# Layer 0 attention: key rank parts in a pool of their own that later holds head 1's operands, head 1 split ahead of the attention loop, rope weights behind each evacuation

## The chip, the cores and the metric

The kernel runs on one core of one Trainium2 chip. The metric is device time in microseconds (us) of one execution. A core has five engines that work side by side and each take their instructions strictly in order: TensorE (PE; its weight loads are listed apart as PEld), VectorE (DVE), ScalarE (ACT), GpSimd (POOL) and SyncE (SP, which here only issues DMA transfers). Matrix products land in PSUM, everything else lives in SBUF, and large arrays stay in HBM.

## The reference

Two decoder layers over 1024 positions of width 1024, each with a token mixer, four memory cross-attention heads beside it, an output projection and a squared-ReLU MLP. The change touches the mixer of layer 0, multi-head latent attention with 12 heads:

```python
proj = hn @ w_in
c_q, c_kv, k_r, q_cross = ...            # ranks 384 and 256, rope key 32, cross queries 256
q = (rmsnorm(c_q, q_norm_g) @ w_uq).reshape(b, s, 12, 96)
q = concatenate([q[..., :64], rope(q[..., 64:], positions)])
kv = (rmsnorm(c_kv, kv_norm_g) @ w_ukv).reshape(b, s, 12, 128)
k_nope, v = kv[..., :64], kv[..., 64:]
k = concatenate([k_nope, broadcast(rope(k_r))])
o = causal_dense_attention(q, k, v)      # softmax(q k / sqrt(96), masked) v
x = x + concatenate([o, cross]) @ w_o
```

## The kernel before

All products are computed at float32 accuracy by splitting each operand into a rounded high part and a residue (`split`: ACT writes the high part, DVE the residue, names ending in h and l) and adding three matmuls: high by high, high by low, low by high. An operand that is "split" therefore costs one ACT and one DVE instruction before PE can use it.

The part around the change, in the order of the program:

- **Input projection and transposes** (`a_in`, `a_cT`). For each of eight token blocks the normalised ranks are transposed by PE, seven blocks of 128 columns and the 32 rope-key columns, into two PSUM tiles `psct`, and split into `cTh`, `cTl`: slices 0 to 2 are the query rank, slices 3 and 4 the rank of keys and values.
- **Values** (`values_of`, PSUM `psv`) and the cross-attention heads.
- **Keys' nope parts** (PSUM `pskn`, six tiles `j` of two heads each, PE lines 118 to 121). A tile is evacuated half by DVE (line 924) and half by ACT (line 925) into `kq`. Two PSUM tiles alternate, so tile `j+2` needs the evacuation of tile `j`. At `j == 1` all nine pieces of the rope weights `wqr` are requested in one go (`load_cols`): SP loads a raw piece `wr` (line 700, two staging buffers), ACT scales it to `wqrh` (line 102), DVE writes the residue `wqrl` (line 103).
- **Rope queries** (`q_rope`, PSUM `psqr`), which need a whole third of `wqr` for each step `kt`, then rotation, transposes `psqt`, and meanwhile the nope weights `wqn`.
- **Query loop** (`q_nope`, PSUM `psqn`, lines 109 to 111), with the row maxima of head 0 in it (`row_max`, PSUM `psx`: PE line 897, DVE lines 901 and 904) and at the end the transpose of the maxima (`max_row`, PSUM `psxt`, PE line 877), whose result becomes row 96 of head 0's query operand.
- **Attention loop**, 12 heads of 12 blocks. A step issues the score matmuls (`pss`, line 1027), the mask on diagonal blocks (DVE line 1035), the exponential `p` (ACT line 1037), for some blocks a split `ph`, `pl`, then the value matmuls `pso` (line 1057) of a block three steps back, with row maxima of the next heads in between. The tables `WHEN` and `ahead` set the order by hand. `masked` holds the last mask and exponential; `tc.issue_after` places what follows behind a given instruction on its engine.
- **Head operands** (`head_tiles(h)`): four loads on SP gather a head's query `q32` and key `k32` (96 rows), which are split into `qh, ql, kh, kl` (lines 99 and 100 as `split` prints them). Three sets `bufs_` rotate over the heads. Set 0 lies in pool `hb`; sets 1 and 2 lie in `hb1`, opened only after the query loop, when `cp` (with `cTh`, `cTl`) and `xq` have been released. So head 1 is split just ahead of the attention loop and head 2 at its seventh step.
- **Denominators**. The last row of `pso` is the sum of a row's probabilities. For groups of 6, 4 and 1 heads (`GRP`), DVE takes the reciprocal (`rc_split`), a DMA writes it out, and `rc_pair` broadcasts it back to 64 partitions a head into `rb`, `[128, 512]` with two buffers: POOL issues these for groups 0 and 1 (line 1109), SP for the last. `rc_mul` multiplies the outputs by it (DVE line 1126). Head 11 is normalised directly from PSUM (`last_o`, reciprocal line 1096 and product line 1097, four pieces).
- **Output projection** (PSUM `pswo`, lines 109 to 111): its stationary operand `x_...` is split per token block, and the first pass needs the high part (L109, L110) before the residue (L111).

The order within an engine comes from a scheduler that places instructions by its own estimate of when they are ready; the order on the chip is then fixed.

Of the kernel before, what the change touches and what calls it, by code (L numbers as in the profile page):

```python
# [19 lines left out]
P = 128  # L20
# [35 lines left out]
def trunk(  # L56
# [670 lines left out]
    def a_cT(t):  # L727
        sl = slice(t * P, (t + 1) * P)
        c = cs_.pop(t)
        pt = [ps1(f"psct{t}_{i}") for i in range(2)]  # L730
        for i in range(7):
            nc.tensor.transpose(pt[i // 4][:, (i % 4) * P : (i % 4 + 1) * P], c[:, i * P : (i + 1) * P], ident)
        nc.tensor.transpose(pt[1][0:32, 3 * P : 4 * P], c[:, CKR : CKR + 32], ident)
        pv = [q.rearrange("p (k c) -> p k c", k=4) for q in pt]
        split(pv[0], cTh[:, 0:4, sl], cTl[:, 0:4, sl])
        split(pv[1][:, 0:1, :], cTh[:, 4:5, sl], cTl[:, 4:5, sl])
        for h in range(4):
            stack_split(pt[1][(h % 2) * 64 : (h % 2) * 64 + 64, (1 + h // 2) * P : (2 + h // 2) * P], qc[:, h, sl], 1.0)
        nc.scalar.activation(krT[:, sl], pt[1][0:32, 3 * P : 4 * P], AF.Copy)

    for k in range(NT + 2):
        if 1 < k < NT:
# [16 lines left out]
    def values_of(t):  # L759
        sl = slice(t * P, (t + 1) * P)  # L760
        ps = [ps1(f"psv{t}_{g}")[:, 0:384] for g in range(2)]
        gs = [slice(g * 384, (g + 1) * 384) for g in range(2)]
        mm3w(ps, [(cTh[:, 3 + kt, sl], cTl[:, 3 + kt, sl], [(wkv[kt][0][:, s], wkv[kt][1][:, s]) for s in gs]) for kt in range(2)])
        nc.scalar.activation(v[:, t, gs[0]], ps[0], AF.Copy)
        nc.vector.tensor_copy(v[:, t, gs[1]], ps[1])

# [144 lines left out]
    krs = raw_tile([32, S], "krs")  # L911
    hb = pool("hb")
    head_bufs(hb, 0)
    head_ones(0)
    nc.vector.tensor_copy(krs, krT)
    for j in range(6):
        if j == 1:
            wqr = rows(wpair(wu, 3, 384, "wqr", "b"), 3)
            for _ in load_cols(mla_w_uq[0], 3, 96, [(wqr, 64, 32)], g_q):
                pass  # L920
        ps = ps2(f"pskn{j}")
        mm3w([ps[:, s] for s in halves],
             [(wkn[kt][0][:, j * P : (j + 1) * P], wkn[kt][1][:, j * P : (j + 1) * P], [(cTh[:, 3 + kt, s], cTl[:, 3 + kt, s]) for s in halves]) for kt in range(2)])
        nc.vector.tensor_copy(kn[j][:, 0:512], ps[:, 0:512])
        nc.scalar.activation(kn[j][:, 512:1024], ps[:, 512:1024], AF.Copy)
# [178 lines left out]

    def rc_pair(c, j, i):

        rb = at.tile([P, 512], F32, tag="rb", bufs=2, name=f"rb{c}_{j}_{i}")
        for e in range(min(2, GRP[c + 1] - GRP[c] - 2 * j)):
            (nc.sync if c == 2 else nc.gpsimd).dma_start(out=rb[e * 64 : e * 64 + 64, :], in_=rc_d[c][2 * j + e, halves[i]].partition_broadcast(64))
        return rb  # L1110

    def rc_split(c):

        n = (GRP[c + 1] - GRP[c]) * NT
        rc = at.tile([48, P], F32, tag="rc", bufs=1, name=f"rc{c}")[:n]
        nc.vector.reciprocal(rc, den[c])
        (nc.sync if c == 2 else nc.gpsimd).dma_start(out=rc_d[c].rearrange("h (t p) -> (h t) p", p=P), in_=rc)
        r_tiles[c] = [(j, i) for j in range((GRP[c + 1] - GRP[c] + 1) // 2) for i in (1, 0)]
        r_tiles[c] = [(j, i, rc_pair(c, j, i)) for j, i in r_tiles[c]]

    def rc_mul(c):

        for j, i, rb in r_tiles.pop(c):
            m = 64 * min(2, GRP[c + 1] - GRP[c] - 2 * j)
            o = qn[GRP[c] // 2 + j][0:m, halves[i]]
            nc.vector.tensor_tensor(o, rb[0:m], o, ALU.mult)
            yield

# [4 lines left out]
    v_tiles(0)  # L1133
    v_full(0)
    mask(wide[0], 1)
    head_tiles(1)

    LV, LB = 3, 5
    NB = len(blocks)
# [60 lines left out]
    at.release()  # L1200
    hb1.release()
    hb.release()
    kvp.release()

# [1106 lines left out]
```

## Time and profile before

| | us |
|---|---|
| median of 3 runs | 2097.34 (2095.71 to 2097.36) |
| the profiled execution | 2098.42 |
| its span (first to last instruction) | 2096.7 |
| PE busy in the span | 2073.6 |
| DVE / ACT / POOL busy | 1473.6 / 1109.1 / 148.9 |
| mean granted TensorE clock | 0.999 |

The stages of the change in this trace: keys' nope parts 175 to 192 us, rope queries 192 to 207, query loop 207 to 235, attention 235 to about 436, output projection from there. A row of the timeline reads: start, duration, engine, line of the kernel, operation, output `<-` inputs by the program's names, shape, count, and in brackets how long the engine had been idle before it and who released it. Since the ends of pipelined matmuls are modelled, the distance between two starts says more than the duration. A row of the table of stretches gives the window, its length, then busy us and count of PE, PEld, DVE, ACT and POOL, the granted clock (1.00 is full), the busy share of the DMA engines and GB/s.

### The profile page before, as it was taken

Reading aid. Unit: us, or ns where it says so; the run is one execution under the profiler, and the core shown is the slowest. Engines: PE = TensorE matmul, PEld = TensorE weight load, DVE = VectorE, ACT = ScalarE, POOL = GpSimd, SP = SyncE. Lnnn points to the kernel's source line nnn. Section 1 sums busy time; section 2 is a strip of 40 time slices with the busy share of each in tenths; the row PEclk is TensorE's granted clock in tenths of the full one; section 3 lists DMA queues with packets and bytes.
Section 4 is the critical chain, followed back from the end, with each engine's and each line's share of the span. In section 5 each row is a group of like instructions: output and inputs, shape, how many; then the busy total and the mean of one; then the engine's idle time right before and its main releaser. Section 6 shows DMA issues by size and latency. Waiting matters only on the chain.

```text
span 2096.7 us, 28899 instructions
## 1 busy us (share of the span) xinstructions
PE 2073.6 (99%) x9744; PEld 1691.1 (81%) x9744; DVE 1473.6 (70%) x2978; ACT 1109.1 (53%) x2396; POOL 148.9 (7%) x265
## 2 busy tenths in 40 slices
PE   8999999999999999999999999999999999999998
PEld 6988777778888888888888878778888888888887
DVE  8766777775977777976658534666977776976565
ACT  7554466656755544444446435776755444444453
POOL 1001001000000000000001133421000000000000
PEclk9999999999999999999999999999999999999999
DMA  6302233342344446944433534542345446945342
GB/s 219 99 1 76 59 69 87 101 147 91 125 153 164 161 146 233 326 140 155 141 116 106 151 92 126 138 138 81 119 163 165 155 141 232 328 148 156 117 120 90
DMA packets 181939, 292.33 MB, mean 139 GB/s; under 512 B 17707, under 2 KB 72096, under 8 KB 181792
## 3 DMA queue, kind: packets, MB, share of 16 engines
q1 hardware_dynamic: 175296, 272.07, 41.4%
q0 software_dynamic: 5168, 15.80, 2.1%
q10 hardware_dynamic: 1328, 2.63, 0.4%
q8 instruction: 76, 1.25, 0.3%
q14 instruction: 71, 0.58, 0.1%
HBM read 187.34 MB, written 81.18 MB: 128 GB/s over the span
## 4 chain that ended last, share of the span: by engine, by line
PE 93%; DVE 3%; ACT 2%; DMA 1%; issue 1%; ACTq 0%; POOL 0%; DVEq 0%
PE psu L1545 6%; PE psu L1547 6%; PE psu L1546 6%; PE psy L1885 6%; PE psy L1884 6%; PE psy L1883 5%; PE psz L1885 4%; PE psz L1884 4%; PE psz L1883 4%; PE psv L1545 4%; PE psv L1547 4%; PE psv L1546 4%; PE pso L1057 3%; PE pswo L109 3%; PE pswo L111 3%; PE pswo L110 3%
## 5 line engine op out<-in xcount | busy, mean ns | idle before, releaser
L99 ACT ACTIVATE g<-i 128x512 fp32r<-128x512 f32 x79 | 49.8, 631 | 103.3 <-PE psy L1884 51.8
L1037 ACT ACTIVATE p<-pss 128x512 f32<-128x512 f32 (+2 forms) x144 | 68.5, 486 | 59.6 <-DVE pss L1035 51.5
L1883 PE MATMUL psy<-g 128*128 128x512 f32 x256 | 100.0, 390 | 0.0
L1884 PE MATMUL psy<-g 128*128 128x512 f32 x256 | 99.7, 389 | 0.0
L1885 PE MATMUL psy<-g 128*128 128x512 f32 x256 | 99.6, 389 | 0.0
L100 DVE TENSOR_TENSOR g<-i,g 128x512 fp32r<-128x512 f32 x79 | 55.3, 700 | 50.2 <-ACT g L99 50.0
L1057 PE MATMUL pso<-p,vf 128*128 128x512 f32 (+3 forms) x214 | 87.9, 492 | 0.3 <-ACT p L1037 0.3
L99 ACT ACTIVATE i<-mr 128x512 fp32r<-128x512 f32 x78 | 47.8, 627 | 73.1 <-PE psu L1546 20.9
L99 ACT ACTIVATE uh<-i 128x512 fp32r<-128x512 f32 x66 | 41.6, 631 | 82.5 <-PE psz L1884 38.3
L100 DVE TENSOR_TENSOR uh<-i,uh 128x512 fp32r<-128x512 f32 x66 | 45.6, 691 | 46.7 <-ACT uh L99 46.7
L904 DVE CUSTOM_DVE_ANT_0 psx<-psx,wide 128x1024 f32<-128x1024 f32 (+6 forms) x88 | 66.7, 760 | 14.2 <-PE psx L897 14.0
L1883 PE MATMUL psz<-g 128*128 128x512 f32 x192 | 74.7, 389 | 0.0
L1884 PE MATMUL psz<-g 128*128 128x512 f32 x192 | 74.7, 389 | 0.0
L1885 PE MATMUL psz<-g 128*128 128x512 f32 x192 | 74.7, 389 | 0.0
L100 DVE TENSOR_TENSOR i<-mr,i 128x512 fp32r<-128x512 f32 x78 | 53.7, 689 | 24.7 <-ACT i L99 24.5
L1444 ACT ACTIVATE mr<-mr,gcol 128x256 f32<-128x256 f32 (+1 forms) x160 | 63.9, 475 | 12.9 <-DMA mr<-in_mlp_w_up_dram 12.9
L1027 PE MATMUL pss<-qh,kh 97*128 97x512 f32 (+2 forms) x144 | 64.4, 448 | 0.3 <-ACT p L1037 0.2
L1027 PE MATMUL pss<-ql,kh 97*128 97x512 f32 (+2 forms) x144 | 61.4, 426 | 0.0
L1765 DVE TENSOR_TENSOR mqq<-mqf,mqq 128x512 f32<-128x512 f32 x64 | 43.2, 688 | 19.6 <-DMA mqf<-in_mlp_w_down_dram 19.6
L1885 PEld LDWEIGHTS psy<-g 128*128 128x128 f32 x256 | 48.1, 188 | 9.9
L1884 PEld LDWEIGHTS psy<-g 128*128 128x128 f32 x256 | 48.1, 188 | 9.9
L1883 PEld LDWEIGHTS psy<-g 128*128 128x128 f32 x256 | 48.1, 188 | 9.8
(662 smaller groups left out, 6838.3 us busy)
## 6 DMA issues: line engine op xcount, KB each, us to landing
i<-hd SPq DMA_DIRECT2D x154, 256.0 KB
hd<-uh SPq DMA_DIRECT2D x76, 256.0 KB
hd<-ul SPq DMA_DIRECT2D x76, 256.0 KB
mr<-in_mlp_w_up_dram SPq DMA_DIRECT2D x36, 512.0 KB
hd<-x SPq DMA_DIRECT2D x72, 256.0 KB
mr<-hd SPq DMA_DIRECT2D x70, 256.0 KB
d<-in_mlp_w_up_dram SPq DMA_DIRECT2D x32, 512.0 KB
mqf<-in_mlp_w_down_dram SPq DMA_DIRECT2D x32, 512.0 KB
```

What stands on the lines that cost most here:

```text
L99: a = nc.scalar.activation(hi, src, AF.Copy)
L100: d = nc.vector.tensor_tensor(lo, src, f32(hi), ALU.subtract)
L904: nc.vector.tensor_tensor_reduce(o, o, k, -1.0, least, ALU.add, ALU.min, accum_out=m)
L1027: return lambda: nc.tensor.matmul(o, a, b, skip_group_check=True, **kw)
L1037: masked[1:] = [nc.scalar.activation(p[:, c0:], ps, AF.Exp, scale=SC).ins]
L1057: mms.append(lambda: nc.tensor.matmul(o, a, b, skip_group_check=True, **kw))
L1545: nc.tensor.matmul(ps, wh[:, k, :], xh[:, k, :], start=p in (1, 2, 5) and k == 0, stop=False, skip_group_check=True)
L1546: nc.tensor.matmul(ps, wh[:, k, :], xl[:, k, :], start=False, stop=False, skip_group_check=True)
L1547: nc.tensor.matmul(ps, wl[:, k, :], xh[:, k, :], start=False, stop=k == 3, skip_group_check=True)
L1883: nc.tensor.matmul(ps, ah[:, j, :], bh, start=start, stop=False, skip_group_check=True)
L1884: nc.tensor.matmul(ps, ah[:, j, :], bl, start=False, stop=False, skip_group_check=True)
L1885: nc.tensor.matmul(ps, al[:, j, :], bh, start=False, stop=k == NP - 1, skip_group_check=True)
```

## The change

- The rank parts of keys and values get a pool `ckv` with `ckh`, `ckl` (two slices each), and `cTh`, `cTl` keep three. `a_cT` groups the transposes as three plus rope key, and four. `values_of` and the key tiles read `ckh`, `ckl`.
- Once the key tiles are done, the four slices of `ckh`, `ckl` serve as head 1's `qh, ql, kh, kl`. Hence `head_tiles(1)` moves into the query loop at `n == 7`. `hb1` holds head 2's set alone; `ckv` and `xq` are released after the attention.
- `head_tiles(2)` moves from step 6 to step 5 of the attention loop, placed behind the mask and exponential of that step.
- The rope weights are no longer requested in one go at `j == 1`, but two pieces behind each ACT evacuation of a key tile.
- `rb` shrinks to 256 columns, still with two buffers, so there are 24 multiplies for 12, and 44 broadcasts for 22.

```diff
+    ckv = pool("ckv", "right")
+    ckh, ckl = [ckv.tile([P, 2, S], F32R, name=f"ck{e}") for e in "hl"]
     cp = pool("cp", "right")
-    cTh = cp.tile([P, 5, S], F32R, name="cTh")
-    cTl = cp.tile([P, 5, S], F32R, name="cTl")
+    cTh = cp.tile([P, 3, S], F32R, name="cTh")
+    cTl = cp.tile([P, 3, S], F32R, name="cTl")
...
-        for i in range(7):
-            nc.tensor.transpose(pt[i // 4][:, (i % 4) * P : (i % 4 + 1) * P], c[:, i * P : (i + 1) * P], ident)
+        at_ = [(0, 0), (0, 1), (0, 2), (1, 0), (1, 1), (1, 2), (1, 3)]
+        for i, (b, o) in enumerate(at_):
+            nc.tensor.transpose(pt[b][:, o * P : (o + 1) * P], c[:, i * P : (i + 1) * P], ident)
...
-        split(pv[0], cTh[:, 0:4, sl], cTl[:, 0:4, sl])
-        split(pv[1][:, 0:1, :], cTh[:, 4:5, sl], cTl[:, 4:5, sl])
+        split(pv[0][:, 0:3, :], cTh[:, :, sl], cTl[:, :, sl])
+        split(pv[1][:, 0:2, :], ckh[:, :, sl], ckl[:, :, sl])
...
     head_bufs(hb, 0)
+    bufs_.append([t[0:97, e, :] for t in (ckh, ckl) for e in range(2)])
     head_ones(0)
...
-        if j == 1:
+        if j == 0:
             wqr = rows(wpair(wu, 3, 384, "wqr", "b"), 3)
-            for _ in load_cols(mla_w_uq[0], 3, 96, [(wqr, 64, 32)], g_q):
-                pass
+            loading = load_cols(mla_w_uq[0], 3, 96, [(wqr, 64, 32)], g_q)
...
         nc.vector.tensor_copy(kn[j][:, 0:512], ps[:, 0:512])
-        nc.scalar.activation(kn[j][:, 512:1024], ps[:, 512:1024], AF.Copy)
+        with tc.issue_after(nc.scalar.activation(kn[j][:, 512:1024], ps[:, 512:1024], AF.Copy).ins):
+            for _ in range(2):
+                next(loading, None)
...
+        if n == 7:
+            head_tiles(1)
         if n == 8:
             max_row(0)
...
-    xq.release()
...
-    for i in (1, 2):
-        head_bufs(hb1, i)
+    head_bufs(hb1, 2)
...
-        rb = at.tile([P, 512], F32, tag="rb", bufs=2, name=f"rb{c}_{j}_{i}")
+        rb = at.tile([P, 256], F32, tag="rb", bufs=2, name=f"rb{c}_{j}_{i}")
...
-        r_tiles[c] = [(j, i) for j in range((GRP[c + 1] - GRP[c] + 1) // 2) for i in (1, 0)]
+        r_tiles[c] = [(j, i) for j in range((GRP[c + 1] - GRP[c] + 1) // 2) for i in (3, 2, 1, 0)]
...
-            o = qn[GRP[c] // 2 + j][0:m, halves[i]]
+            o = qn[GRP[c] // 2 + j][0:m, i * 256 : i * 256 + 256]
...
-    head_tiles(1)
...
-            if j == (0 if h else 6) and h + 2 < H:
+            if h and j == 0 and h + 2 < H:
                 head_tiles(h + 2)
+            if n == 5:
+                with tc.issue_after(masked[0]), tc.issue_after(masked[1]):
+                    head_tiles(2)
...
     hb1.release()
+    ckv.release()
+    xq.release()
```

Three places show how the instructions stand on DVE. The first is the end of head 0's row maxima in the query loop (`psx0_7` is the last block of maxima, `ckh ... <-q32_1` head 1's query residue, `mhl0` the split of the transposed maxima). Before:

```order
433 L934 COPY qn0_1928<-psqn3_1_2429 128x512
434 L901 TENSOR_REDUCE m8_0_2349<-psx0_7_2413 128x1
435 L904 ISA psx0_7_2413,m8_0_2349<-psx0_7_2413,dmask_66,m8_0_2349 128x128
436 L904 ISA m8_0_2349 128x1
437 L100 TENSOR_TENSOR mhl0_2453<-psxt0_2451,mhl0_2453 8x128
```

And in the changed kernel:

```order
431 L939 COPY qn0_1933<-psqn3_1_2434 128x512
432 L904 TENSOR_REDUCE m8_0_2354<-psx0_7_2418 128x1
433 L100 TENSOR_TENSOR ckh_551<-q32_1_2445,ckh_551 96x1024
434 L907 ISA psx0_7_2418,m8_0_2354<-psx0_7_2418,dmask_66,m8_0_2354 128x128
435 L907 ISA m8_0_2354 128x1
436 L100 TENSOR_TENSOR mhl0_2470<-psxt0_2468,mhl0_2470 8x128
```

The residue of head 1's query now stands between the reduction and the masked maximum of the last block. The second place is the first steps of the attention loop. Before:

```order
441 L1130 COPY vf_2518<-v 128x8x64
442 L100 TENSOR_TENSOR ql_2503<-q_1_2536,qh_2502 96x1024
443 L100 TENSOR_TENSOR kl_2505<-k_1_2537,kh_2504 96x1024
444 L1035 TENSOR_TENSOR pss_0_0_2554<-pss_0_0_2554,dmaskT 128x128
...
462 L100 TENSOR_TENSOR pl_0_2_2615<-p_0_2_2612,ph_0_2_2614 128x256
463 L1000 TENSOR_TENSOR vl_2517<-v,vh_2516 128x256
464 L100 TENSOR_TENSOR ql_2507<-q_2_2636,qh_2506 96x1024
465 L100 TENSOR_TENSOR kl_2509<-k_2_2637,kh_2508 96x1024
466 L1035 TENSOR_TENSOR pss_0_3_2651<-pss_0_3_2651,dmaskT 128x128
```

And in the changed kernel:

```order
440 L1135 COPY vf_2530<-v 128x8x64
441 L1040 TENSOR_TENSOR pss_0_0_2554<-pss_0_0_2554,dmaskT 128x128
...
457 L907 ISA psx_5_2641,m_1_2572<-psx_5_2641,wide 128x768
458 L907 ISA m_1_2572 128x1
459 L100 TENSOR_TENSOR ql_2519<-q_2_2621,qh_2518 96x1024
460 L100 TENSOR_TENSOR pl_0_2_2615<-p_0_2_2612,ph_0_2_2614 128x256
461 L100 TENSOR_TENSOR kl_2521<-k_2_2622,kh_2520 96x1024
462 L1005 TENSOR_TENSOR vl_2529<-v,vh_2528 128x256
463 L1040 TENSOR_TENSOR pss_0_3_2651<-pss_0_3_2651,dmaskT 128x128
```

Head 1's two residues are gone from the start; head 2's two stand a little earlier, still ahead of the mask of block `pss_0_3`. The third place is the end of head 11, where its output is normalised (`rq`, `fa`) and the first operand of the output projection (`x_0_3`) is split. Before:

```order
829 L1096 RECIPROCAL rq_4576<-pso_1_4487 64x128
830 L100 TENSOR_TENSOR x_0_3_4637<-qn_1928,x_0_3_4637 128x512
831 L1097 TENSOR_TENSOR fa_101<-pso_1_4487,rq_4576 64x128
832 L1096 RECIPROCAL rq_4576<-pso_1_4487 64x128
833 L100 TENSOR_TENSOR x_0_3_4637<-fa_101,x_0_3_4637 128x256
```

And in the changed kernel:

```order
837 L1102 TENSOR_TENSOR fa_101<-pso_1_4523,rq_4617 64x128
838 L1101 RECIPROCAL rq_4617<-pso_1_4523 64x128
839 L1131 TENSOR_TENSOR fa_101<-rb_0_1_4567,fa_101 64x256
840 L1102 TENSOR_TENSOR fa_101<-pso_1_4523,rq_4617 64x128
841 L1131 TENSOR_TENSOR fa_101<-rb_0_0_4569,fa_101 64x256
842 L100 TENSOR_TENSOR x_0_3_4685<-qn_1933,x_0_3_4685 128x512
843 L100 TENSOR_TENSOR x_0_3_4685<-fa_101,x_0_3_4685 128x256
```

The first residue of `x_0_3` moved behind the last reciprocal, and two of the narrow multiplies stand ahead of it.

More of the change, by code (lines that the diff above doesn't have):

```diff
@@ L730, in a_cT @@
         pt = [ps1(f"psct{t}_{i}") for i in range(2)]
[L731 to L733 removed]
+        at_ = [(0, 0), (0, 1), (0, 2), (1, 0), (1, 1), (1, 2), (1, 3)]
+        for i, (b, o) in enumerate(at_):
+            nc.tensor.transpose(pt[b][:, o * P : (o + 1) * P], c[:, i * P : (i + 1) * P], ident)
+        nc.tensor.transpose(pt[0][0:32, 3 * P : 4 * P], c[:, CKR : CKR + 32], ident)
         pv = [q.rearrange("p (k c) -> p k c", k=4) for q in pt]
[L735 to L736 removed]
+        split(pv[0][:, 0:3, :], cTh[:, :, sl], cTl[:, :, sl])
+        split(pv[1][:, 0:2, :], ckh[:, :, sl], ckl[:, :, sl])
         for h in range(4):
[L738 to L739 removed]
+            stack_split(pt[1][(h % 2) * 64 : (h % 2) * 64 + 64, (2 + h // 2) * P : (3 + h // 2) * P], qc[:, h, sl], 1.0)
+        nc.scalar.activation(krT[:, sl], pt[0][0:32, 3 * P : 4 * P], AF.Copy)
     for k in range(NT + 2):
@@ L762, in values_of @@
         gs = [slice(g * 384, (g + 1) * 384) for g in range(2)]
-        mm3w(ps, [(cTh[:, 3 + kt, sl], cTl[:, 3 + kt, sl], [(wkv[kt][0][:, s], wkv[kt][1][:, s]) for s in gs]) for kt in range(2)])
+        mm3w(ps, [(ckh[:, kt, sl], ckl[:, kt, sl], [(wkv[kt][0][:, s], wkv[kt][1][:, s]) for s in gs]) for kt in range(2)])
         nc.scalar.activation(v[:, t, gs[0]], ps[0], AF.Copy)
@@ L916, in trunk @@
     for j in range(6):
-        if j == 1:
+        if j == 0:
             wqr = rows(wpair(wu, 3, 384, "wqr", "b"), 3)
-            for _ in load_cols(mla_w_uq[0], 3, 96, [(wqr, 64, 32)], g_q):
-                pass
+            loading = load_cols(mla_w_uq[0], 3, 96, [(wqr, 64, 32)], g_q)
         ps = ps2(f"pskn{j}")
         mm3w([ps[:, s] for s in halves],
-             [(wkn[kt][0][:, j * P : (j + 1) * P], wkn[kt][1][:, j * P : (j + 1) * P], [(cTh[:, 3 + kt, s], cTl[:, 3 + kt, s]) for s in halves]) for kt in range(2)])
+             [(wkn[kt][0][:, j * P : (j + 1) * P], wkn[kt][1][:, j * P : (j + 1) * P], [(ckh[:, kt, s], ckl[:, kt, s]) for s in halves]) for kt in range(2)])
         nc.vector.tensor_copy(kn[j][:, 0:512], ps[:, 0:512])
-        nc.scalar.activation(kn[j][:, 512:1024], ps[:, 512:1024], AF.Copy)
+        with tc.issue_after(nc.scalar.activation(kn[j][:, 512:1024], ps[:, 512:1024], AF.Copy).ins):
+            for _ in range(2):
+                next(loading, None)
     wu2 = pool("wu2", "right")
@@ L1105, in rc_pair @@
     def rc_pair(c, j, i):
-        rb = at.tile([P, 512], F32, tag="rb", bufs=2, name=f"rb{c}_{j}_{i}")
+        rb = at.tile([P, 256], F32, tag="rb", bufs=2, name=f"rb{c}_{j}_{i}")
         for e in range(min(2, GRP[c + 1] - GRP[c] - 2 * j)):
-            (nc.sync if c == 2 else nc.gpsimd).dma_start(out=rb[e * 64 : e * 64 + 64, :], in_=rc_d[c][2 * j + e, halves[i]].partition_broadcast(64))
+            (nc.sync if c == 2 else nc.gpsimd).dma_start(out=rb[e * 64 : e * 64 + 64, :], in_=rc_d[c][2 * j + e, i * 256 : i * 256 + 256].partition_broadcast(64))
         return rb
```

## The prediction

> **What bounds the kernel now.** I read the busy table first, then the chain of waits, then the table of stretches, then TensorE's rows wherever its starts stand further apart than its work asks.
>
> ```profile
> PE 2073.6 (99%) x9744; PEld 1691.1 (81%) x9744; DVE 1473.6 (70%) x2978; ACT 1109.1 (53%) x2396; POOL 148.9 (7%) x265
> PE 93%; DVE 3%; ACT 2%; DMA 1%; issue 1%; ACTq 0%; POOL 0%; DVEq 0%
> ...
> 234.70:250.70 16.00, 13.90 (x68) 10.37 (x67) 15.62 (x35) 10.37 (x20) 2.21 (x5) 1.00 0.32 76
> 435.00:445.00 10.00, 9.13 (x35) 6.38 (x34) 9.66 (x21) 7.69 (x18) 0.00 (x0) 0.83 0.62 228
> ```
>
> TensorE (PE) is busy for 99% of a span of 2096.7 us and holds 93% of the chain. The change takes no matmul away, so it can only move PE's holes. The third and fourth rows are the two stretches in which VectorE (DVE, the fifth figure) is nearly full (15.62 of 16.00 us, 9.66 of 10.00) and PE is not: the start of attention and its end. All terms below are hole sizes, and each hole is the distance between two PE starts less the distance that such a matmul normally has. That normal distance is 0.23 us for 512 columns (191.25 to 191.48 in the rows below) and 0.17 for 384.
>
> **Part A: rope weights behind each evacuation.**
>
> ```profile
> 186.58 0.50 PE L118 MATMUL pskn<-cTh,wknh 128*128 128x512 f32 x1 [1.09 <-ACT kq L925]
> 191.25 0.39 PE L118 MATMUL pskn<-cTh,wknh 128*128 128x512 f32 x1
> 191.48 0.39 PE L119 MATMUL pskn<-cTl,wknh 128*128 128x512 f32 x1
> ...
> 192.16 0.33 PE L109 MATMUL psqr<-wqrh,cTh 128*128 128x384 f32 x1
> 192.33 0.34 PE L110 MATMUL psqr<-wqrl,cTh 128*128 128x384 f32 x1
> ```
> ```profile
> 185.65 0.40 ACT L102 ACTIVATE wqrh<-wr,gcol 128x128 fp32r<-128x128 f32 x1 [1.89 <-DMA wr<-in_mla_w_uq_dram]
> 185.95 0.58 ACT L925 ACTIVATE kq<-pskn 128x512 f32<-128x512 f32 x1
> ...
> 191.66 0.33 SPq L700 DMA_DIRECT2D wr<-in_mla_w_uq_dram  x1
> 193.95 0.51 ACT L102 ACTIVATE wqnh<-wr,gcol 128x256 fp32r<-128x256 f32 x1 [0.27 <-DMA wr<-in_mla_w_uq_dram]
> ...
> 182.69 1.06 ACT L99 ACTIVATE kh<-k 96x1024 fp32r<-96x1024 f32 x1 [0.68 <-DMA k<-kq]
> ```
>
> Today ScalarE (ACT) stands 1.89 us in front of a rope-weight piece that has not landed, the evacuation of a key tile queues behind it, and PE loses about 1.1 us at 186.58. In the change the evacuations come first, so this hole should go: −1.1. The price is that the nine pieces start behind the first evacuation of a key tile instead of ahead of all of them, with only two staging buffers. A piece needs its load (issued 191.66, used 193.95: 2.3 us, the shortest I see; pieces that queue take up to about 3), a 0.40 us scaling on ACT, and a 0.35 us residue on DVE before the buffer is free again.
>
> The late one is the last piece. In the change ACT first splits head 1's key into the rank parts' own space, which PE reads until its last pskn matmul, about 190.8 (192.16 less the hole, less one more matmul). That split takes 1.06 us, the seventh and eighth piece stand behind it on ACT, the ninth can be loaded only when the seventh's residue is done: 190.8 + 1.06 + 0.40 + 0.35 = 192.6, load issued, 2.6 us on its way, 0.40 scaling: about 195.6. PE starts the rope queries at about 190.9 and first runs the two finished thirds for three token blocks, 18 matmuls of 0.17 us, until 194.0. So it waits about 1.6 us for the third. **A: −1.1 + 1.6 = +0.5.** Bounds: −1.1 if the load is early enough, +2.0 if the ninth piece takes 3.2 us and its residue is waited for too. What is late next is the nope weights, by the same 2 to 3 us; but the rope queries stand in front of their first use (90 matmuls' work on PE in that stage), so I cost that at nothing; if that cover is gone it is at most the same 2 us again. The regrouped transposes are the same eight and the same 640 columns in two evacuations: nothing.
>
> **Part B: head 1 is split inside the query loop.**
>
> ```profile
> 226.85 1.09 DVE L901 TENSOR_REDUCE m<-psx 128x1 f32<-128x896 f32 x1
> 227.98 0.36 DVE L904 CUSTOM_DVE_ANT_0 psx<-psx,dmask,m 128x128 f32<-128x128 f32 x1
> ...
> 228.03 0.39 PE L111 MATMUL psqn<-cTh,wqn2l 128*128 128x512 f32 x1
> 228.46 0.27 PE L877 MATMUL psxt<-ident,m 128*8 128x128 f32 x1
> ...
> 237.91 1.21 DVE L100 TENSOR_TENSOR kl<-k,kh 96x1024 fp32r<-96x1024 f32 x1
> ```
>
> The transpose of head 0's maxima (228.46) already starts 0.2 us late: it needs the masked maximum that DVE begins at 227.98. The change puts head 1's query residue, the same shape as the 1.21 us row, exactly between the reduction and that mask. PE executes in order, and its order is unchanged here, so the next query matmuls wait behind the transpose: **+1.2**, bounds 0 (the piece slips into idle DVE time before the reduction) and +1.3. Its four loads and two row copies also move forward on SyncE's queue, between loads of rope weights; each load takes that queue 0.33 us (191.66), and I cost the two row copies, which wait for the rank parts to be free, within A's bounds.
>
> **Part C: start of attention.**
>
> ```profile
> 236.56 0.39 PE L1027 MATMUL pss<-qh,kl 97*128 97x512 f32 x1
> 237.29 0.73 PE L897 MATMUL psx<-kh,qh 96*128 96x512 f32 x2 [0.34 <-ACT kh L99]
> ...
> 239.84 0.33 PE L1027 MATMUL pss<-qh,kl 97*128 97x384 f32 x1
> 240.50 0.70 PE L1057 MATMUL pso<-p,vf 128*128 128x512 f32 x1 [0.32 <-ACT p L1037]
> ...
> 247.45 0.47 PE L1057 MATMUL pso<-pl,vh 128*128 128x256 f32 x1
> 249.30 0.33 PE L897 MATMUL psx<-kh,qh 96*128 96x128 f32 x1 [1.38 <-ACT p L1037]
> ```
> ```profile
> 236.69 1.29 DVE L100 TENSOR_TENSOR ql<-q,qh 96x1024 fp32r<-96x1024 f32 x1
> ...
> 246.38 1.21 DVE L100 TENSOR_TENSOR ql<-q,qh 96x1024 fp32r<-96x1024 f32 x1
> 247.51 1.21 DVE L100 TENSOR_TENSOR kl<-k,kh 96x1024 fp32r<-96x1024 f32 x1
> 248.65 0.29 DVE L1035 TENSOR_TENSOR pss<-pss,dmaskT 128x128 f32<-128x128 f32 x1
> ```
>
> The holes are 0.5 us (236.56 to 237.29, less 0.23), 0.5 us (239.84 to 240.50, less 0.17) and about 1.6 us (247.45 to 249.30). The first two are head 1's own splits, the third is the mask at 248.65 standing behind head 2's. The change takes 1.29 + 1.21 = 2.5 us of DVE work (and as much of ACT) out of a stretch in which DVE never rests. Head 2's stay but start earlier, each behind one more short operation, so the backlog at 247 should be 2.5 us smaller and a hole of 1.6 can close. The sum of holes is 2.6; I take **−2.3**, as head 2's splits may still leave a rest of the third. Bounds: −2.6 (all three close) and −1.0 (only the first two, since head 2's splits still stand before that mask).
>
> **Part D: the denominators in pieces of 256 columns.**
>
> ```profile
> L1109 POOL DMA_DIRECT2D rb<-rcd x20: 516/523/732, 349.2 to 423.1; - x20
> ...
> DMA to landing us min/median/max: 2.7/2.9/3.4
> ```
> ```profile
> 353.15 0.69 DVE L1126 TENSOR_TENSOR qn<-rb,qn 128x512 f32<-128x512 f32 x1 [2.27 <-DMA rb<-rcd]
> ...
> 364.94 0.69 DVE L1126 TENSOR_TENSOR qn<-rb,qn 128x512 f32<-128x512 f32 x1 [0.70 <-DMA rb<-rcd]
> ...
> 246.04 0.42 DVE L1000 TENSOR_TENSOR vl<-v,vh 128x256 fp32r<-128x256 f32 x1
> ...
> 367.08 0.68 PE L897 MATMUL psx<-kh,qh 96*128 96x512 f32 x2 [0.93 <-DVE m L904]
> ```
>
> Twelve multiplies of 0.69 us become 24 of about 0.42 (the row at 246.04 has that width): 12 × (0.84 − 0.69) = 1.8 us more DVE work, spread over 74 us of a kernel in which DVE is busy for 70%. POOL issues 40 broadcasts of 0.52 instead of 20, in a stretch where it is nearly empty. The real cost is the round trip: still two buffers, so each piece waits for the multiply two before it, then 2 × 0.52 of issue and 2.9 of flight, 4 us; DVE waits in order, with masks queued behind it. Before, the waits at 353.15 and 364.94 are such ones, and PE's 0.93 at 367.08 follows the second. From the pace of the masks I expect four further DVE waits of 0.3 to 1.2 us in group 0, one directly ahead of a row-maximum that PE waits for. **D: +0.5**, bounds 0 and +1.5.
>
> **Part E: end of the last head.**
>
> ```profile
> 440.43 0.63 PE L110 MATMUL pswo<-woq,x 128*128 128x512 f32 x1
> 440.86 0.63 PE L111 MATMUL pswo<-woq,x 128*128 128x512 f32 x1
> ...
> 439.80 0.62 DVE L100 TENSOR_TENSOR x<-qn,x 128x512 fp32r<-128x512 f32 x1
> 440.45 0.28 DVE L1097 TENSOR_TENSOR fa<-pso,rq 64x128 f32<-64x128 f32 x1
> 440.77 0.96 DVE L1096 RECIPROCAL rq<-pso 64x128 f32<-64x128 f32 x1
> ```
>
> The first L111 matmul (440.86) needs the residue of the first output-projection tile, which DVE finishes at 440.42. In the change it stands behind the fourth reciprocal (0.96), two products (0.28 each) and two of the four narrow multiplies (0.42 each). Added to 439.80, less what overlaps, it ends at about 442.4, so PE waits **+1.6** at that matmul. Bounds: +0.8 (PE runs here at half rate, 0.43 us from start to start, and a hole inside the slow stretch costs half) and +3.3 (a clock of 0.83 over 10 us is 3.4 us at half rate, so 1.7 us lost, and the hole brings that once more).
>
> The row of the ten microseconds from 435 shows a mean granted clock of 0.83, whereas the stretch with the 1.6 us hole at 248 keeps 1.00, so a longer hole alone doesn't lower it. The Trainium skill ("TensorE: Matmul & The Clock Gate", section "Part 1: The HAM clock gate") says that the clock halves after an idle window of about 3.4 us and returns after as long a busy one. By that rule a hole of 1.6 us slows nothing, as at 248, and E is the hole itself; the slow ten microseconds after 435, in which PE was busy for 9.13, don't fit it.
>
> **The sum.** A +0.5, B +1.2, C −2.3, D +0.5, E +1.6: **+1.5 us**. The profiled execution took 2098.42 us, 1.1 above the median of 2097.34 of the runs shown; a hole costs both the same, so I forecast 2097.34 + 1.5 = **2098.8 us**. Lower bounds of all five together give −2.9 (−1.1, 0, −2.6, 0, +0.8), upper ones +7.1 (2.0, 1.3, −1.0, 1.5, 3.3).
>
> **Rivals.**
> 1. *The gain stays.* The start of attention closes wholly and the other places absorb their delays: DVE is idle for 30% of the span. −1.1 in A with no late ninth piece, B and D nothing, C −2.6, E +0.8: −2.9, 2094.4. Against it: B and E sit where PE already waits, so nothing covers them. Chance 0.12.
> 2. *The clock at the end decides (slower).* If the wait at the first L111 falls before the clock has recovered, another stretch at half rate follows, and each costs the 1.7 us worked out above. With two of them, E is 1.6 + 3.4 = 5.0 and the sum 1.5 + 3.4 = +4.9, 2102.2. [...] For it: the clock does fall here today; against: 248 shows such a hole without a fall. Chance 0.14.
> 3. *The broadcasts' round trip.* Twelve more pieces with two buffers: if half of them hold a mask up for 1 us that PE then waits for, D is +6 and the sum +7.0, 2104.3. Against: of the two DVE waits quoted, 2.27 and 0.70 us, only the shorter one has a PE hole behind it. Chance 0.10.
> 4. *It doesn't do what it says.* Head 1's splits only move from one place where PE waits for DVE to another (B eats C), and the rope weights bring their own hole. This is nearly my sum; with C at −1.0 it is +2.8, 2100.1, still inside what counts as no change. I count it with the forecast.
>
> **How the numbers follow.** A difference of 0.2%, 4.2 us, is about what a measurement of this kernel can tell from no change. Forecast with rival 4: 0.64, all within. Rival 1 (0.12) ends 1.3 us inside the lower edge; small holes that I don't list carry it over in half of the cases, and the rest of it is no change: 0.07 faster. Rival 2 (0.14) lies just beyond the upper edge: 0.10 slower, 0.04 no change. Rival 3 is slower with all its 0.10. So faster 0.07, same 0.73, slower 0.20. The range takes in rivals 1 and 2, and not rival 3: 2093.5 to 2103.5.
>
> **What would show it.** In the changed profile: no wait of pskn for the evacuation near 186, but one of psqr for a rope weight near 194; the transpose of the maxima about 1.2 us after the matmul ahead of it; PE starts 0.17 to 0.23 apart between 236 and 250; a multiply waiting for its broadcast ahead of a row maximum between 350 and 375; the first L111 of the output projection 1 to 2 us later relative to the L110 ahead of it. I am wrong if PE's holes between 175 and 250 shrink by over 3 us in all, or if those after 435 grow by over 4.

## The result, and the profile after

The change makes the kernel slower: median 2106.99 us (2103.74 to 2107.54, six runs) against 2096.7 us (2095.66 to 2097.6, six runs) of the kernel before, a ratio of 1.0045 with a 95% interval of 1.0035 to 1.0056. The forecast was 2098.8, the range ended at 2103.5. The profiled execution took 2106.43 us with a span of 2104.6, 7.9 more than the span of 2096.7 before. The medians differ by 10.3: the profiled execution before was itself 1.7 us above the median of that kernel in this comparison, and the profiled one of the change 0.6 below its own.

The page of the changed kernel, its busy table and its chain of waits:

```profile
PE 2075.8 (99%) x9744; PEld 1692.1 (80%) x9744; DVE 1472.8 (70%) x2990; ACT 1108.7 (53%) x2396; POOL 158.6 (8%) x285
...
PE 91%; DVE 3%; DMA 3%; ACT 2%; issue 1%; POOL 0%; ACTq 0%; DVEq 0%; SPq 0%; POOLq 0%
```

PE has the same matmuls, and DVE about the same work. PE's share of the chain fell from 93% to 91% and DMA's rose from 1% to 3%. So the time went into waits that end with a transfer. The table of what PE waited for, in the changed kernel (total us, times, longest):

```profile
PE psx L900 <- DVE m L907: 4.2, 3, 2.9
PE pswo L111 <- DVE x L100: 1.7, 1, 1.7
PE pso L1062 <- ACT ph L99: 1.5, 2, 1.0
PE psqt L957 <- POOL fa L332: 1.3, 1, 1.3
...
PE psxt L880 <- DVE m L907: 1.0, 1, 1.0
```

The longest wait of the kernel, 2.9 us for a row maximum, is in no term of the prediction at that size. Here it is, in PE's timeline of the changed kernel, 383 to 391 us:

```profile
383.66 0.39 PE L1032 MATMUL pss<-qh,kl 97*128 97x512 f32 x1
386.90 0.68 PE L900 MATMUL psx<-ckl,ckh 96*128 96x512 f32 x2 [2.85 <-DVE m L907]
...
391.15 0.40 PE L1032 MATMUL pss<-qh,kl 97*128 97x512 f32 x1
```

The same three matmuls in the kernel before:

```profile
383.21 0.39 PE L1027 MATMUL pss<-qh,kl 97*128 97x512 f32 x1
383.56 0.68 PE L897 MATMUL psx<-kh,qh 96*128 96x512 f32 x2
...
386.25 0.39 PE L1027 MATMUL pss<-qh,kl 97*128 97x512 f32 x1
```

The first distance grew from 0.35 to 3.24 us, the second from 2.69 to 4.25: 2.9 us of waiting, and then 1.6 us more for the same work. Why PE waited is in DVE's timeline of the changed kernel:

```profile
381.89 0.43 DVE L1131 TENSOR_TENSOR qn<-rb,qn 128x256 f32<-128x256 f32 x1 [0.68 <-DMA rb<-rcd]
...
385.02 0.43 DVE L1131 TENSOR_TENSOR qn<-rb,qn 128x256 f32<-128x256 f32 x1 [2.37 <-issue]
385.36 0.29 DVE L1040 TENSOR_TENSOR pss<-pss,dmaskT 128x128 f32<-128x128 f32 x1
385.56 1.22 DVE L907 CUSTOM_DVE_ANT_0 psx<-psx,wide 128x1024 f32<-128x1024 f32 x1
```

DVE stands 2.37 us in front of a narrow multiply. Behind it queue a mask and the row maximum at 385.56 that PE needs. The row names no releaser ("issue"), so the cause has to be read elsewhere: in the timelines of the POOL and SP queues, and in the last row of the table for the tile `rb`, which gives the time from a broadcast's issue to its landing.

```profile
378.09 2.06 POOL L1114 DMA_DIRECT2D rb<-rcd  x4 [6.25 <-DVE qn L1131]
...
378.64 0.53 SPq L797 DMA_DIRECT2D wor<-in_w_o_dram  x1
```
```profile
DMA to landing us min/median/max: 2.4/2.5/5.3
```

POOL could issue four broadcasts only when an earlier multiply had freed the buffers. Between them SP issued the load of a piece of the output weights (`wor`, 128 x 1024 float32, 512 KB). Before the change no broadcast took over 3.4 us; now one takes 5.3, and the six that POOL issues between 378 and 384 us have a median of 4.4, though each is only half as large. The last of the four was issued at about 379.6 (378.09 + 2.06 − 0.52); 5.3 us later it is 384.9, and the multiply starts at 385.02.

The 1.6 us behind the hole are the clock, in the table of stretches of the changed kernel:

```profile
383.00:387.50 4.50, 1.65 (x10) 1.12 (x9) 2.33 (x6) 1.65 (x4) 0.64 (x2) 1.00 0.56 175
387.50:391.50 4.00, 4.00 (x15) 3.36 (x14) 2.63 (x4) 1.56 (x4) 0.00 (x0) 0.57 0.01 2
391.50:395.00 3.50, 3.50 (x14) 2.22 (x13) 3.07 (x4) 3.50 (x5) 0.00 (x0) 1.00 0.62 186
```

After the hole PE is always busy, but the granted clock is 0.57 over 4 us: 0.43 × 4 × 2 = 3.4 us at half rate, which loses 1.7 us of work.

### The profile page after: what moved, and what is told of

Its sections match the earlier page's. It is cut to its first block, busy times and chain, and to the rows that moved or that the text cites. A ratio compares the mean times of both kernels' runs of the same rounds, so it can differ in the third digit from the quotient of the medians.

```text
span 2104.6 us, 28950 instructions
## 1 busy us (share of the span) xinstructions
PE 2075.8 (99%) x9744; PEld 1692.1 (80%) x9744; DVE 1472.8 (70%) x2990; ACT 1108.7 (53%) x2396; POOL 158.6 (8%) x285
## 4 chain that ended last, share of the span: by engine, by line
PE 91%; DVE 3%; DMA 3%; ACT 2%; issue 1%; POOL 0%; ACTq 0%; DVEq 0%; SPq 0%; POOLq 0%
PE psy L1894 5%; PE psy L1892 5%; PE psy L1893 5%; PE psu L1556 5%; PE psu L1554 5%; PE psu L1555 5%; PE psz L1894 4%; PE psz L1892 4%; PE psz L1893 4%; PE psv L1554 4%; PE psv L1555 4%; PE psv L1556 4%; PE pswo L111 3%; PE pswo L109 3%; PE pswo L110 3%; PE pso L1062 3%
## 5 line engine op out<-in xcount | busy, mean ns | idle before, releaser
L1453 ACT ACTIVATE d<-d,gcol 128x256 f32<-128x256 f32 x128 | 53.6, 497 | 0.1
L2149 ACT ACTIVATE sp<-sp,sst 128x257 f32<-128x257 f32 (+1 forms) x96 | 46.5, 487 | 13.1 <-DVE sst L2147 12.5
```

The costliest lines, as they stand in the source:

```text
L1453: nc.scalar.activation(w[:, k, :], w[:, k, :], AF.Copy, scale=g_mlp[layer][:, k0 + k : k0 + k + 1])
```

## The experiments

Two theories stood after this reading. **Narrow pieces**: nearly the whole loss comes from `rb` at 256 columns with two buffers, which together hold half of what they held. **The rest**: the loss is spread over the moved splits, the rope weights and the end. The kernel before had a median of 2096.8 us in both comparisons below (21 and 31 runs).

**Only the narrow pieces, in the kernel before.**

```diff
-        rb = at.tile([P, 512], F32, tag="rb", bufs=2, name=f"rb{c}_{j}_{i}")
+        rb = at.tile([P, 256], F32, tag="rb", bufs=2, name=f"rb{c}_{j}_{i}")
...
-        r_tiles[c] = [(j, i) for j in range((GRP[c + 1] - GRP[c] + 1) // 2) for i in (1, 0)]
+        r_tiles[c] = [(j, i) for j in range((GRP[c + 1] - GRP[c] + 1) // 2) for i in (3, 2, 1, 0)]
```

> The kernel before with one part of the change alone: broadcasts and multiplies of the denominators in pieces of 256 columns, two buffers. Theory 'round trip' (each piece waits for the multiply two before it, then two issues and the flight; masks stand behind it on DVE): the loss at heads 9 and 11 comes with it, +4 to +7 us, 2101 to 2104, with a TensorE hole behind a row maximum near 380 and a later first L111 near 440. Rival 'preparation' (the loss comes from the rope weights and head 1's early split): 0 to +1, at most 2098. Rival 'accident' (a w_o load met a broadcast only because the rest of the change had shifted the time): +1 to +3, with no hole over 1 us near 380.

Measured: 2107.11 us (2106.8 to 2108.31), ratio 1.005 (1.0037 to 1.0063). This edit alone costs 10.3 us, as much as the whole change and more than the 4 to 7 that were expected. Its timelines of DVE and of PE show a hole in the same place, and this time the row names the transfer:

```profile
383.21 0.42 DVE L1126 TENSOR_TENSOR qn<-rb,qn 128x256 f32<-128x256 f32 x1 [2.12 <-DMA rb<-rcd]
...
385.09 0.67 PE L897 MATMUL psx<-kh,qh 96*128 96x512 f32 x2 [2.40 <-DVE m L904]
```

That hole is not the whole loss. By the distances of matching PE starts, 3.0 us are lost in this run by 400 us, and about 5 more around the end of head 11 and the start of the output projection, where the clock falls (table of stretches of this kernel):

```profile
437.00:445.00 8.00, 5.97 (x22) 3.39 (x21) 6.82 (x16) 6.32 (x18) 0.00 (x0) 0.81 0.51 142
445.00:453.00 8.00, 7.28 (x19) 5.23 (x19) 7.81 (x17) 4.76 (x8) 0.00 (x0) 0.55 0.71 248
```

These two rows hold (0.19 + 0.45) × 8 × 2 = 10.2 us at half rate. The kernel before had 3.4 there (0.79 over the 8 us from 437 to 445), so there are 6.8 us more at half rate, and they make up 3.4 of these 5 us.

**The change with the wide pieces**, 512 columns twice. Room for them comes from one buffer for the split maxima instead of two and from a shared tile for the denominators.

```diff
-            mh, ml = [at.tile([8, P], F32R, tag=f"m{e}", bufs=2, name=f"m{e}{h}") for e in "hl"]
+            mh, ml = [at.tile([8, P], F32R, tag=f"m{e}", bufs=1, name=f"m{e}{h}") for e in "hl"]
...
-    den = [at.tile([(b - a) * NT, P], F32, name=f"den{a}") for a, b in zip(GRP, GRP[1:])]
+    den = [at.tile([n, P], F32, name=f"den{a}") for a, n in ((0, 48), (6, 40))]
+    den = [den[0], den[1][0:32], den[1][32:40]]
...
-        rb = at.tile([P, 256], F32, tag="rb", bufs=2, name=f"rb{c}_{j}_{i}")
+        rb = at.tile([P, 512], F32, tag="rb", bufs=2, name=f"rb{c}_{j}_{i}")
...
-        rc = at.tile([48, P], F32, tag="rc", bufs=1, name=f"rc{c}")[:n]
+        rc = den[c]
```

> The changed kernel with the denominators back in pieces of 512 columns, two buffers; the 2 KB come from one buffer instead of two for the split maxima, sums of the last group beside the group before, and the reciprocal written in place. Theory 'round trip': 2099.5 to 2102 (5 to 7 us less than the changed kernel), the 2.85 us hole behind the row maximum near 384 gone and the first L111 within 0.6 us of its place relative to the kernel before. Rival 'preparation': 2105 to 2107, as the hole only moves.

Measured: 2098.01 us (2096.65 to 2099.78, 11 runs), ratio 1.0006 (0.9997 to 1.0014), better than the theory asked for. All other parts of the change together cost 1.2 us or nothing. With the run before, both directions agree: narrow pieces cost 10.3 us in the old kernel and 9.0 (2106.99 − 2098.01) in the new one.

**Narrow pieces with four buffers**, in the same room. This asks whether the number of pieces or the distance ahead decides.

```diff
-        rb = at.tile([P, 256], F32, tag="rb", bufs=2, name=f"rb{c}_{j}_{i}")
+        rb = at.tile([P, 256], F32, tag="rb", bufs=4, name=f"rb{c}_{j}_{i}")
```

> The changed kernel with pieces of 256 columns but four buffers, room as in the run with 512 columns. Theory 'round trip': what counts is how far ahead the broadcasts run; four of half the size run as far ahead as two of the full size, so 2100 to 2102.5. Rival 'number of pieces' (twice as many multiplies and broadcasts cost by themselves, whatever the buffers): 2105 to 2107, as the changed kernel.

Measured: 2100.95 us (2098.59 to 2102.73, 11 runs), ratio 1.0019 (1.001 to 1.0028). The hole at 384 is gone with 24 narrow multiplies still there, so it is the distance ahead. The times of issue say the same: the last broadcast of group 0 leaves POOL at 368.5 us here and at 366.4 in the kernel before, about ten us ahead of the first weight load (378.0 and 378.3); in the change it leaves at 383.1, and the first weight load at 378.6. What remains over the wide version, 2.9 us, has its largest piece at the end, in PE's timeline of this kernel:

```profile
442.86 0.76 PE L111 MATMUL pswo<-woq,x 128*128 128x512 f32 x1 [1.78 <-DVE x L100]
```

This is the wait that part E forecast; with wide pieces no wait is listed at that matmul. Behind it this kernel has 3.4 us at half rate (a clock of 0.87 from 437 to 445 us and of 0.92 from 445 to 453), the wide version none.

**Is it the weight load beside the broadcasts?** The first two output-weight loads are held back until later blocks, by a one-element write into their buffer that stands behind a later mask.

```diff
             raw = self.raw[j] = raw_tile([P, 2, 512], f"wor{layer}_{half}_{j}")
+            if layer == 0 and half == 0 and j < 2:
+                nc.vector.memset(raw[0:1, 0, 0:1], 0.0)
...
-            wq.step()
+            with tc.issue_after(masked[0]), tc.issue_after(masked[1]):
+                wq.step()
```

> The changed kernel with the first two loads of output weights (512 KB each) held back by a one-element write into their buffers that stands behind a later mask; all broadcasts stay in place. Theory 'contention' (the broadcast that landed after 5.3 us shared the DMA engines with such a load): it lands in about 2.5 us, the hole of 2.85 us at 384 and the slow clock behind it go: 3.5 to 4.5 us less, about 2103. Rival 'two buffers alone' (the wait is the chain of buffer, issue and flight): the hole stays over 2 us, 2106 to 2107.5. Either may lose up to 1.5 us at 420 to 440, where the held-back weights now come closer.

Measured: 2102.49 us (2101.4 to 2103.51, nine runs), ratio 1.0027 (1.0017 to 1.0037), 4.5 us under the change. DVE and PE of this kernel at the old hole, and then both where a new one opened:

```profile
381.76 0.42 DVE L1133 TENSOR_TENSOR qn<-rb,qn 128x256 f32<-128x256 f32 x1
...
383.63 0.67 PE L902 MATMUL psx<-ckl,ckh 96*128 96x512 f32 x2 [0.18 <-DVE m L909]
...
435.53 0.85 DVE L1133 TENSOR_TENSOR fa<-rb,fa 128x256 f32<-128x256 f32 x2 [2.24 <-DMA rb<-rcd]
...
438.45 0.44 PE L1064 MATMUL pso<-ph,vh 128*128 128x384 f32 x1 [2.90 <-ACT ph L99]
```

Without the load beside it the multiply doesn't wait, and PE waits 0.18 us instead of 2.85. The hole comes back where a held-back weight load meets a later pair of broadcasts, in the timelines of SP and POOL, with the last row of the table for `rb` in this kernel:

```profile
429.10 0.38 SPq L799 DMA_DIRECT2D wor<-in_w_o_dram  x1
429.96 1.03 POOL L1116 DMA_DIRECT2D rb<-rcd  x2 [0.70 <-DVE fa L1133]
DMA to landing us min/median/max: 2.4/2.6/5.0
```

The second of the pair leaves at 430.47 (429.96 + 1.03 − 0.52) and 5.0 us later it is 435.47; the multiply that needs it starts at 435.53. One run thus shows the cause twice. The Trainium skill ("DMA: Bandwidth & Descriptors", section "Issuing engines are not separate DMA queues") says that transfers issued by different engines run on the same sixteen DMA engines and interleave. The trace agrees, with up to 5.3 us for a broadcast that takes 2.5 in the median. The prediction didn't ask which other queue was busy.

**Head 1's splits behind the transpose of the maxima**, for part B, and for the cause that part A gave (the key split ahead of the seventh rope piece on ACT).

```diff
-        split(pt, mh, ml)
+        done = split(pt, mh, ml)
...
+        return done
...
-        if n == 7:
-            head_tiles(1)
         if n == 8:
-            max_row(0)
+            maxed = max_row(0)
+            with tc.issue_after(maxed[0]), tc.issue_after(maxed[1]):
+                head_tiles(1)
```

> The changed kernel with head 1's operands split behind the split of head 0's maxima instead of in front of its last masked maximum. Theory: the transpose of the maxima starts on time again (-1.0), and since head 1's key split no longer stands on ScalarE in front of the seventh rope-weight piece, the holes of 0.9 and 1.4 us at the rope queries shrink too (-1 to -2.3); 2103 to 2105, near -3. Rival 'rope loads': the rope hole is the late loads alone and stays: 2105.5 to 2106.5. Rival 'moved': the splits now delay the last query evacuation and the first scores by as much: 2106 to 2107.5.

Measured: 2105.38 us (2103.58 to 2107.28, five runs), ratio 1.004 (1.0028 to 1.0053), 0.4 above the range of the theory. The interval overlaps that of the change, so the time alone tells little; the trace does. The transpose of the maxima starts without its wait of 1.0 us (229.53, against 230.75), which confirms B. The rope weights don't move, as ACT's timeline of this kernel shows:

```profile
191.06 0.40 ACT L102 ACTIVATE wqrh<-wr,gcol 128x128 fp32r<-128x128 f32 x1 [0.21 <-DMA wr<-in_mla_w_uq_dram]
...
194.19 0.40 ACT L102 ACTIVATE wqrh<-wr,gcol 128x128 fp32r<-128x128 f32 x1 [2.08 <-DMA wr<-in_mla_w_uq_dram]
```

With the split out of the way, the last piece still comes at 194.19 (194.42 in the change): what is late is its load, not ACT's queue. The load went out at 191.77, when the residue of an earlier piece, which DVE began at 191.40 behind an evacuation, had freed one of the two staging buffers. So part A's chain of two buffers held, and its cause for the delay fell: the key split took no time out of it.

**Both together**: wide pieces, and head 1 behind the transpose.

> Denominators in pieces of 512 columns and head 1 split behind the split of head 0's maxima, all else as in the changed kernel. Theory (terms add up): 2098.0 of the run with 512 columns, less 1.1 for the transpose of the maxima: 2096.9, within 1 us of the kernel before; the holes at the rope queries (1.2 and 1.6 us) and the 1.0 us ahead of the first scores stay. Rival (the loss moves): 2098 again.

Measured: 2096.78 us (2095.73 to 2099.72, 11 runs), ratio 1.0001 (0.9992 to 1.001). That is what was expected if the two repairs add up, though the gain of 1.2 us over the wide version alone is within the intervals.

**And the rope weights in one go at the second key tile**, as before the change.

```diff
-        if j == 0:
+        if j == 1:
             wqr = rows(wpair(wu, 3, 384, "wqr", "b"), 3)
-            loading = load_cols(mla_w_uq[0], 3, 96, [(wqr, 64, 32)], g_q)
+            for _ in load_cols(mla_w_uq[0], 3, 96, [(wqr, 64, 32)], g_q):
+                pass
...
-        with tc.issue_after(nc.scalar.activation(kn[j][:, 512:1024], ps[:, 512:1024], AF.Copy).ins):
-            for _ in range(2):
-                next(loading, None)
+        nc.scalar.activation(kn[j][:, 512:1024], ps[:, 512:1024], AF.Copy)
```

> As the run before, and the rope weights requested in one go at the second key tile as in the kernel before. Theory (the rope holes are the late loads with two staging buffers): holes of 1.2 and 1.6 us gone, the 0.9 us of the evacuation back, and the first scores take another PSUM tile, one that ScalarE empties earlier, so their 1.0 us goes too: 2094.0 to 2095.5, faster than the kernel before. Rival (the rope holes come from head 1's row copies or splits): no better than the run before, 2096.5 to 2097.5.

Measured: 2093.3 us (2091.83 to 2095.05, 11 runs), ratio 0.9984 (0.9975 to 0.9993): a little faster than both kernels, and than expected. The waits of the rope queries (A) and of the first score matmul (below) are gone, and the old wait for the evacuation came back only as a rest, in PE's timeline:

```profile
185.24 0.50 PE L118 MATMUL pskn<-ckh,wknh 128*128 128x512 f32 x1 [0.24 <-ACT kq L930]
```

**The first two pieces ahead of the first evacuation**, the others behind each: a compromise of both orders.

```diff
             loading = load_cols(mla_w_uq[0], 3, 96, [(wqr, 64, 32)], g_q)
+            next(loading)
+            next(loading)
```

> As the run with both repairs, the rope weights still two pieces behind each evacuation, but the first two pieces ahead of the first evacuation, so that the whole chain starts some 4 us earlier. Theory (late loads): neither the rope holes nor the hole of the evacuation: 2093.0 to 2094.5, the best of all. Rival (the evacuation hole returns, as ScalarE waits for pieces again): 2094.5 to 2096.

Measured: 2094.73 us (2092.71 to 2096.98, 11 runs), ratio 0.9991 (0.9982 to 1.0), just above the theory's range and inside the rival's. The rival's wait did not return: both old waits are gone, but a nope weight took the place of the rope weight, in the timelines of ACT and PE of this kernel:

```profile
207.47 0.51 ACT L102 ACTIVATE wqn2h<-wr,gcol 128x256 fp32r<-128x256 f32 x1 [3.14 <-DMA wr<-in_mla_w_uq_dram]
...
208.87 0.50 PE L109 MATMUL psqn<-cTh,wqnh 128*128 128x512 f32 x1 [0.81 <-ACT qr L962]
```

An evacuation (`qr`) queued on ACT behind a weight that hadn't landed: the same pattern as at 186.58 in the kernel before, one stage later.

## Why the prediction was wrong, by its steps

Measured from the distances of matching PE starts in the two profiled executions (times of the changed kernel); the terms add up to the 7.9 us of the spans, with 0.4 us gained ahead of the first one:

| part | predicted | measured |
|---|---|---|
| A, rope weights | +0.5 | +1.6 (−1.1 at `pskn`, +1.1 at `psqr`, +1.6 at `psqt`) |
| B, transpose of the maxima | +1.2 | +1.1 |
| first score matmul | not in the sum | +1.0 |
| C, start of attention, to 269 us | −2.3 | −2.0 |
| D, pieces of 256 columns, 269 to 391 us | +0.5 | +3.6 (−0.9 by 368, then +4.5) |
| E, from 391 us to the end | +1.6 | +3.0 |

The gain of 0.9 us by 368 belongs to D: the kernel before with the narrow pieces alone shows the same 0.9 there, and the wide version does not. The rows down to C, with the 0.4, come to +1.3, which agrees with the 1.2 us that the wide version measured for all parts but D and E.

**D is the step that failed.** Of the 6.4 us by which the spans exceed the forecast of +1.5, it has 3.1; E has 1.4, A 1.1 and the first score matmul 1.0. D took 0.5, bounded it at 1.5, and gave rival 3, this very round trip, a chance of 0.10. The mechanism was there: two buffers, four microseconds a round, DVE waiting in order with masks behind it. Mis-sized was the term "four further DVE waits of 0.3 to 1.2 us". The flight of 2.9 us was taken from the median of broadcasts beside which no weight load ran. The runs showed one flight of 5.3 us beside a weight load (+2.9), and a clock that fell behind that hole (+1.6). Rival 3's price, 2104.3, was nearest to the truth, but its picture was not: in D's stretch not six waits of 1 us each, but one of 2.9 us. Rival 2, more half-rate stretches at the end, is not what the change shows there (0.79 over the 8 us from 445 to 453, as before over those from 437 to 445), but it is what the kernel with only the narrow pieces shows. Two buffers of 512 columns let the broadcasts run far enough ahead to end before the weight loads begin; at half the size they are still under way when those come.

**E was half right**, within its bound of +3.3. The wait at the first L111 came as worked out, 1.7 us, behind the narrow multiplies:

```profile
446.94 0.39 PE L110 MATMUL pswo<-woq,x 128*128 128x512 f32 x1
449.05 0.70 PE L111 MATMUL pswo<-woq,x 128*128 128x512 f32 x1 [1.72 <-DVE x L100]
```

Ahead of it lies what the part left out: the last broadcasts of group 1 still arrive while head 11's blocks run. In the changed kernel's timelines of DVE and PE:

```profile
437.51 0.42 DVE L1131 TENSOR_TENSOR fa<-rb,fa 128x256 f32<-128x256 f32 x1 [0.81 <-DMA rb<-rcd]
437.86 0.29 DVE L1040 TENSOR_TENSOR pss<-pss,dmaskT 128x128 f32<-128x128 f32 x1
...
441.51 0.44 PE L1062 MATMUL pso<-ph,vh 128*128 128x384 f32 x1 [0.98 <-ACT ph L99]
```

The mask at 437.86 stands behind such a multiply. Its exponential, its split and the next block's follow it, and PE waits 0.98 us for a `ph`. This is D's round trip again, after the stretch for which D was costed, and here without a weight load beside it: the four broadcasts that POOL issues from 433.2 on land in 2.4 to 2.5 us.

**A was within its bounds, in part by luck**: the hole of 1.1 at `pskn` closed as forecast, the one at `psqr` was 1.1 us where 1.6 was forecast, and 1.6 at `psqt` was not in the sum. Timelines of PE and ACT in the changed kernel:

```profile
193.84 0.34 PE L111 MATMUL psqr<-wqrh,cTl 128*128 128x384 f32 x1
194.88 0.79 PE L109 MATMUL psqr<-wqrh,cTh 128*128 128x384 f32 x3 [0.70 <-ACT wqrh L102]
...
198.05 0.55 PE L957 MATMUL psqt<-ident,fa 128*128 128x128 f32 x3 [1.32 <-POOL fa L332]
...
194.42 0.40 ACT L102 ACTIVATE wqrh<-wr,gcol 128x128 fp32r<-128x128 f32 x1 [2.03 <-DMA wr<-in_mla_w_uq_dram]
```

The 18 matmuls of the two finished thirds did end at 194.0, as worked out, and the last piece came a little earlier than the 195.6 of the prediction. But running two thirds of three token blocks first means that no block is finished until the last third is there. Their rotation on DVE and POOL then has no cover, and the transposes wait 1.32 us for it. The prediction saw the order and did not ask what waits for a finished block.

**B and C were right** (+1.1 for +1.2, −2.0 for −2.3); B's row is the query residue in front of the masked maximum, in DVE's timeline of the changed kernel:

```profile
228.14 1.09 DVE L904 TENSOR_REDUCE m<-psx 128x1 f32<-128x896 f32 x1
229.15 1.21 DVE L100 TENSOR_TENSOR ckh<-q,ckh 96x1024 fp32r<-96x1024 f32 x1
230.28 0.35 DVE L907 CUSTOM_DVE_ANT_0 psx<-psx,dmask,m 128x128 f32<-128x128 f32 x1
```

In C, of the third hole a wait of 0.62 us at 250.79 is left where there was one of 1.38.

**Not foreseen** was a wait at the first score matmul, PE and DVE of the changed kernel:

```profile
236.80 0.39 PE L111 MATMUL psqn<-cTh,wqn2l 128*128 128x512 f32 x1
238.04 0.50 PE L1032 MATMUL pss<-qh,kh 97*128 97x512 f32 x1 [0.85 <-DVE fa L939]
...
237.30 0.69 DVE L939 COPY fa<-psqn 128x512 f32<-128x512 f32 x1 [3.46 <-PE psqn L111]
```

The matmul waits for the copy of the last query tile, and the likely reason is that the first score tile lies in that tile's PSUM space. The kernel before and the version with both repairs and the rope weights in one go show no wait here, and for the second this was forecast. What places the tile so in each was not tried by itself.

## What to carry to other kernels

When buffers shrink, cost not only the extra instructions but how far the transfers run ahead: list what else is in flight when the late ones are, on all queues, since a flight time read from quiet rows need not hold beside a large load (2.5 us became 4.4 to 5.3 here). A multiply that could wait for a transfer does its harm through what stands behind it on its engine, so placing it behind the mask and the row maximum is worth a try; no run here tried it. When a weight arrives late and matmuls are regrouped around it, ask what needs the first finished result, not only whether PE has work.

## What the runs showed of the hardware

A hole in PE's work of 2.85 us (the change, at 384) and one of 2.90 us (the held-back loads, at 435) were each followed by about 3.4 us at half clock; a hole of 2.40 us in the kernel with only the narrow pieces was not. The table of stretches of that last kernel, behind its hole, and then of the kernel with held-back loads:

```profile
385.00:390.00 5.00, 3.82 (x19) 3.02 (x20) 3.27 (x8) 3.82 (x8) 0.00 (x0) 1.00 0.13 33
```
```profile
437.00:445.00 8.00, 5.38 (x18) 3.66 (x18) 7.67 (x17) 6.25 (x17) 0.00 (x0) 0.79 0.14 25
```

The last row gives 0.21 × 8 × 2 = 3.4 us at half clock again, so each of these two holes cost about 1.6 us on top of its length. The length alone need not be what decides. Stretches cut to the clock's own switches, two of the change and one of the kernel with only the narrow pieces:

```profile
387.74:391.15 3.41, 3.41 (x13) 2.84 (x12) 2.45 (x4) 1.17 (x3) 0.00 (x0) 0.50 0.00 0
449.18:452.59 3.41, 3.41 (x9) 2.64 (x10) 3.38 (x9) 2.36 (x4) 0.00 (x0) 0.50 0.93 354
```
```profile
441.90:452.14 10.24, 8.91 (x23) 5.99 (x22) 9.93 (x22) 7.82 (x16) 0.00 (x0) 0.50 0.85 277
```

The half-rate stretches are 3.41 us long or three times that, and the two of the change begin 61.44 us apart, 18 times 3.41. So the clock seems to be set once in each step of a fixed grid of 3.41 us. Counted back in such steps from 441.90, a boundary lies at 383.88 us, in the middle of the hole of 2.40 us (382.69 to 385.09). Of the change's 2.85 us, which end at 386.90, 2.57 lie in the one step that ends at 387.74. That the place on the grid saved the shorter hole is an inference from these few holes; no run moved a hole on the grid. The Trainium skill ("TensorE: Matmul & The Clock Gate", section "Part 1: The HAM clock gate") gives an idle window of about 3.4 us for the fall and as long a busy one for the return. The return agrees; the fall came here after steps that were not idle throughout (PE was busy for 0.84 of the 3.41 us up to 387.74 in the change). In the wide version the stretch from 437 to 445 us keeps a clock of 1.00 with four waits of 0.2 to 0.7 us in it, where the kernel before fell to half clock at 439.30 with shorter ones; what measure of activity decides stays open.
